# A trunk of two layers: rounded transposes from word copies at the layer boundaries and in three more MLP clusters

## The chip, the cores and the metric

One core of one Trainium2 chip runs the whole kernel in one launch. The metric is the device time of one execution in microseconds (us), as the median of several runs. Engines: TensorE (PE), its weight loads (PEld), VectorE (DVE), ScalarE (ACT), GpSimd (POOL), SyncE (SP).

## The reference

256 tokens of width 2048 go through two layers in fp32. Each layer is a mixer (latent attention, MLA, in the first; a state space mixer, SSM, in the second) and a squared-ReLU MLP of width 8192, each behind an RMS norm and added to the residual:

```python
def squared_relu_mlp(h, w_in, w_out):
    u = jax.nn.relu(h @ w_in)
    return (u * u) @ w_out

for i in range(DEPTH):
    h = rms_norm(x, mix_norm_g[i])
    mix = mla_mixer(h, ...) if i % N_MIXERS == 0 else ssm_mixer(h, ...)
    x = x + mix
    h = rms_norm(x, mlp_norm_g[i])
    x = x + squared_relu_mlp(h, mlp_w_in[i], mlp_w_out[i])
```

## The kernel before

**Products.** The 256 tokens are two row tiles (t = 0, 1) of 128. Every fp32 product is made of three fp32r matmuls of 128x512: each operand is split into a rounded part h (ScalarE's copy, L299 for activations and L102 for weights) and the rest lo (VectorE's subtraction, L300 and L103). A weight unit is 128x1024: SyncE loads it into a `wraw` buffer (6 of them), L102 and L103 make `wh` and `wl` (4 each), and twelve matmuls use it. `Flow` loads some units ahead and splits three ahead. A matmul needs the contracted dimension on the partitions, so each activation block is transposed on TensorE: four transposes of 128x128 into one PSUM bank (a cluster, `transposed`, L307), then L299 and L300.

**The two kinds of transposes.** L315 transposes fp32 data against an fp32 identity, `ident`. L313 transposes fp32r data (`words`) against the fp32r identity `identr`. For the latter, the first 384 columns of the block are copied, bytes unchanged, by a DMA of GpSimd's queue into an fp32r tile `tr` (L559); the fourth transpose stays fp32. Before, only MLP pairs 1 to 6 do this (`WORDS`).

**Boundaries.** There are three: MLA to MLP, MLP to SSM, SSM to MLP. A product's output comes in four column blocks (nb = 0 to 3). `finalize` adds a block to the residual (L399), multiplies it by the next norm's gain into a scratch tile xg (L401), takes the square sum on ScalarE (L296), and puts the transposes of xg into a queue with `later`. `tick` runs once per output block, that is about once per two weight units, and emits what has come due; `later(0)` is the next tick. At MLA to MLP and MLP to SSM the clusters alternate between two `yp` and two `sm` banks; at SSM to MLP they use `sm` alone (two banks). Column block 3 is the last of a boundary.

**The MLP.** Pairs 0 to 7 of hidden blocks (p): pair 0 is computed as it stands, pairs 1 to 7 by seven products of sums (`seven`). A pair gives four clusters (p, j, t): hidden block j of the pair, row tile t. The order of the units is a list made by `plan` and `merged`; the body walks it and counts estimated TensorE time in `at[0]`. `turn` puts a cluster into `due` at the earliest of its own delay (`TR`, plus `COPY` = 8 for a cluster with a copy) and at least `TR_GAP` = 4 us after the cluster before it. `move` emits the clusters that are due. After the last unit, `move(1e9)` emits all that are left. Then the four output blocks of pair 7 follow (`block`, matmuls L330, L331, L334), which end in `finalize`. `combinations` makes sums of the transposed input for the seven products (`xf`, L513 and L523) and splits them (`sN5`, `sN7`, `sN6`). `seven` adds raw weight tiles on VectorE (L183) and in HBM-to-buffer loads that accumulate on GpSimd's queue (L199). All other matmuls of the MLP are L605, L606, L607; L424 adds an output block to the residual in `x`.

Of the kernel before, what the change touches and what calls it, by code (L numbers as in the profile page):

```python
# [20 lines left out]
F32 = mybir.dt.float32  # L21
F32R = mybir.dt.float32r
# [6 lines left out]
P = 128  # L29
# [9 lines left out]
NEG = -1.0e30  # L39
MAGIC = 12582912.0  # L40

C_ID, C_G0, C_GQ, C_GK, C_MQ, C_TRI, C_SEL = 0, 128, 144, 336, 528, 656, 784
C_INV, C_DTB, C_ALOG, C_CW, C_CB, C_END = 848, 880, 944, 1008, 1200, 1248


def inv_two_pi_parts():
# [168 lines left out]
class Trunk:  # L215
# [82 lines left out]
    def split_out(self, h, lo, src):  # L298
        self.nc.scalar.activation(h, src, AF.Copy)  # L299
        self.nc.vector.tensor_tensor(lo, src, h.bitcast(F32), ALU.subtract)  # L300

    def transposes(self, src, h, lo, t, wide=True):

        sl = slice(t * P, (t + 1) * P)
        self.transposed(src, h[:, :, sl], lo[:, :, sl], wide)

    def transposed(self, src, h, lo, wide=True):  # L307
        b = self.bank(wide)
        src, words = src if isinstance(src, tuple) else (src, None)
        for j in range(4):  # L310
            v = slice(j * P, (j + 1) * P)
            if words is not None and j < 3:
                self.nc.tensor.transpose(b.bitcast(F32R)[:, v], words[:, v], self.ident_r)  # L313
            else:
                self.nc.tensor.transpose(b[:, v], src[:, v], self.ident)  # L315
        self.split_out(h, lo, b.rearrange("p (k n) -> p k n", k=4))
# [67 lines left out]
    def finalize(self, nb, accs, wide=True):  # L384
        nc = self.nc
        g = self.gain_tile(self.nx_gain[nb])
        if not self.by_tile:
            self.nx[nb] = (self.ktile(self.xtp), self.ktile(self.xtp))
        elif nb % 2 == 0:
            for t in range(2):  # L390
                self.nx[nb // 2, t] = [self.ktile(self.xtp).rearrange("p a b -> p (a b)").rearrange("p (k n) -> p k n", n=P)
                                       for _ in range(2)]
        for t in range(2):
            if self.by_tile:
                h, lo = (v[:, 4 * (nb % 2):4 * (nb % 2) + 4] for v in self.nx[nb // 2, t])
            else:
                h, lo = (v[:, :, t * P:(t + 1) * P] for v in self.nx[nb])
            x = self.x[t][nb]
            nc.vector.tensor_tensor(x, accs[t], x, ALU.add)  # L399
            xg = self.scratch()  # L400
            nc.vector.tensor_tensor(xg, x, g, ALU.mult)  # L401
            self.square_sum(x, self.nx_ssq[:, t * 4 + nb:t * 4 + nb + 1])
            self.later(0, lambda h=h, lo=lo, xg=xg: self.transposed(xg, h, lo, wide))

    def boundary_end(self):

# [20 lines left out]
    def start(self, seq):  # L427
        nc, d = self.nc, self.d
        self.flow = Flow(nc, self.wp, seq, (6, 3))
        cst = self.c.tile([P, C_END], F32, name="cst")  # L430
        self.cst = cst
        self.ident = cst[:, C_ID:C_ID + P]
        self.mhalf = self.c.tile([P, 16], F32, name="mhalf")
        warm = self.s2.tile([P, 512], F32R, tag="s2", name="warm")
        nc.vector.memset(warm.bitcast(F32), 1.0)
        bank = self.sm.tile([P, 512], F32, tag="sm", name="warmed")
        for _ in range(WARM):
            nc.tensor.matmul(bank, warm[:, :P], warm, start=True, stop=True)
        nc.gpsimd.memset(self.mhalf, -0.5)
        nc.scalar.dma_start(cst[:, C_G0:C_GQ], d["cst"][:, C_G0:C_GQ])  # L440
        nc.scalar.activation(self.stat(1), self.mhalf[:, :1], AF.Copy)
        raws = [self.ktile(self.k4, F32) for _ in range(4)]
        parts = [(0, slice(k, k + 1)) for k in range(4)] + [(1, slice(0, 2)), (1, slice(2, 4)), (2, slice(0, 4)), (3, slice(0, 4))]

        def some_x():
            j, k = parts.pop(0)
            nc.sync.dma_start(raws[j][:, k], d["xT"][j][:, k])

        self.flow.load(2, ((0, 512), (512, 1024)), some_x)
        for u in range(3, 7):  # L450
            some_x()
            self.flow.load(u)
        self.pos = self.c.tile([P, 2], I32, name="pos")
        self.x = [[self.res.tile([P, 512], F32, name=f"x{t}{n}") for n in range(4)] for t in range(2)]

        self.rs_pool = [self.c.tile([P, 4], F32, name=f"rs{i}") for i in range(2)]
        self.phase = 0
        self.xT = [(self.ktile(self.xtp), self.ktile(self.xtp)) for _ in range(4)]

        def split_x(j, ks):  # L460
            h, lo = self.xT[j]
            for k in ks:
                g = cst[:, C_G0 + 4 * j + k:C_G0 + 4 * j + k + 1]
                if (j, k) == (0, 0):
                    nc.vector.tensor_scalar(h[:, k], raws[j][:, k], g, None, ALU.mult)
                else:
                    nc.scalar.activation(h[:, k], raws[j][:, k], AF.Copy, scale=g)
                nc.vector.scalar_tensor_tensor(lo[:, k], raws[j][:, k], g, h[:, k].bitcast(F32), ALU.mult, ALU.subtract)  # L468

        split_x(0, (0,))  # L470
        self.flow.convert(1)
        split_x(0, (1, 2))
        self.flow.convert(2)
        split_x(0, (3,))
        self.flow.load(7)
        nc.sync.dma_start(cst[:, :C_G0], d["cst"][:, :C_G0])
        nc.sync.dma_start(cst[:, C_GQ:], d["cst"][:, C_GQ:])
        nc.sync.dma_start(self.pos, d["pos"])
        split_x(1, range(4))
        ssq = self.stat(8)  # L480
        self.later(0, lambda: split_x(2, range(4)))
        self.later(1, lambda: split_x(3, range(4)))

        def stats(n):
            for t in range(2):
                nc.sync.dma_start(self.x[t][n], d["x"][t * P:(t + 1) * P, n * 512:(n + 1) * 512])
                self.square_sum(self.x[t][n], ssq[:, t * 4 + n:t * 4 + n + 1])
            if n == 3:
                self.set_rstd(ssq)

        for n, at in enumerate(X_AT):
            self.later(at, lambda n=n: stats(n))
# [51 lines left out]
    def mlp_body(self, mp, layer, gain):  # L544
        nc = self.nc
        xa, rs = self.xT, self.rs
        us = {}
        self.ident_r = mp.tile([P, P], F32R, name="identr")
        nc.gpsimd.tensor_copy(self.ident_r, self.ident)

        def hidden(r, pp, j, t):

            nc.scalar.activation(r, r, AF.Square)
            if (pp, j) not in us:
                us[pp, j] = (self.ktile(self.k4), self.ktile(self.k4))
            h, lo = us[pp, j]
            if pp in WORDS:
                q = mp.tile([P, 384], F32R, tag="tr", name=self.name("tr"), bufs=4)
                nc.gpsimd.dma_start(q.bitcast(F32), r[:, :384])  # L559
                r = (r, q)  # L560
            return lambda wide: self.transposes(r, h, lo, t, wide)

        def relu(src, t):
# [14 lines left out]
        at = [0.0, 0.0]  # L578
# [10 lines left out]
        def turn(r, p, j, t, us):  # L589

            fn = hidden(r, p, j, t)
            at[1] = max(at[0] + us + (COPY if p in WORDS else 0), at[1] + TR_GAP)
            due.append((at[1], lambda: fn(False)))

        def pair_of_banks(pool):
# [49 lines left out]
        for tok in tokens:  # L645
            key = (tok[0], layer) + tok[1:]
            if tok[0] == "s":
                _, p, name, d = tok
# [3 lines left out]
                if count.setdefault(name, 0) % 4 == 0:  # L652
                    pool = self.sm if name == "N7" else self.acc
# [7 lines left out]
            elif tok[0] == "c":  # L661
                _, p, j, o = tok
# [11 lines left out]
            else:  # L674
                _, p, nb, o = tok
# [701 lines left out]
LATE5 = ()  # L1377
TR = (10, 8, 7, 7, 5)
TR_GAP = 4
WORDS = range(1, 7)  # L1380
COPY = 8
PAUSE = 2.7


def merged(p, blocks):
# [21 lines left out]
    while main or late or second or units:  # L1407
        op = next((q for q in (late, main, second) if q and ready(*q[0])), None)
        filler = t >= rest and len(units) > (4 if p == 7 and op else 0)
        if filler and (op is None or work > t * ve / pe - 2):  # L1410
# [3 lines left out]
            if not units or units[0][0] != b:  # L1414
                rest, work = t + (PAUSE if b[0] == "o" else 10), work + 1.37
        else:
# [160 lines left out]
```

## Time and profile before

| | |
|---|---|
| three runs | 2288.47, 2289.15, 2289.5 us; median 2289.15 |
| profiled execution | own time 2289.32 us, span 2287.5 us, clock 1.0 |
| fp32 transposes (L315) | 288, of these 252 into `sm` and 36 into `yp` |
| word transposes (L313) | 144, from 48 copies of 192 KB |
| DMA | 547.52 MB, mean 239 GB/s |

In the profile, a row of the timeline gives the start, the length, the engine, the line, the operation, output<-input and how many instructions in a row it groups (x4); in brackets stands the idle time before it and what ended it. A matmul's length reaches into the next one's, since they are pipelined: the pace is the distance of their starts. Rows of a view by source line give the count, then minimum, median and maximum duration in ns.

### The profile page before, as it was taken

The page shows a single profiled execution, that of the slowest core. Times are in us where ns is not written, and L with a number is a line of the kernel's source. Part 1 is how long each engine was busy: PE and PEld are TensorE (multiplying, and loading weights), DVE is VectorE, ACT ScalarE, POOL GpSimd, SP SyncE. Part 2 cuts the span into 40 slices and gives each one's busy share as a digit, 9 for nine tenths or more (in the row PEclk, how much of TensorE's full clock was granted, in tenths as well). Part 3 has the DMA queues.
Part 4 walks back from the last instruction along what each step waited for, and adds up shares of the span by engine and source line. Part 5 has one row for each costly group of instructions (what it writes and reads, how often), then busy time and mean ns, then how long its engine had stood idle before and what let it go on. Part 6 is the DMA issues. An engine that isn't in the chain of part 4 may idle for free.

```text
span 2287.5 us, 30624 instructions
## 1 busy us (share of the span) xinstructions
PE 2280.0 (100%) x10929; PEld 1893.7 (83%) x10929; DVE 1906.0 (83%) x2318; ACT 1391.2 (61%) x1947; POOL 243.0 (11%) x279
## 2 busy tenths in 40 slices
PE   9999999999999999999999999999999999999999
PEld 7898888888888888888888888888888888888887
DVE  7785698999898897687888688676989989989985
ACT  7775476566566666564666555544666666666663
POOL 1430000000000000000133112110000000000000
PEclk9999999999999999999999999999999999999999
DMA  8435678888888878667877777666688888888875
GB/s 316 151 125 152 202 228 266 261 257 267 265 253 259 268 231 271 202 207 241 279 270 261 251 265 259 221 200 202 208 266 240 267 269 253 261 277 244 267 230 161
DMA packets 164985, 547.52 MB, mean 239 GB/s; under 512 B 18448, under 2 KB 27600, under 8 KB 163808
## 3 DMA queue, kind: packets, MB, share of 16 engines
q1 hardware_dynamic: 151264, 502.44, 66.4%
q0 software_dynamic: 11168, 38.85, 9.0%
q10 hardware_dynamic: 2400, 4.27, 0.5%
q8 instruction: 86, 1.41, 0.2%
q14 instruction: 67, 0.55, 0.1%
HBM read 529.65 MB, written 6.41 MB: 234 GB/s over the span
## 4 chain that ended last, share of the span: by engine, by line
PE 95%; DVE 2%; DMA 2%; ACT 1%; issue 1%; POOL 0%; SPq 0%; ACTq 0%; DVEq 0%
PE acc L330 13%; PE acc L331 13%; PE acc L334 13%; PE yp L606 9%; PE yp L607 9%; PE yp L605 9%; PE st L606 7%; PE st L607 7%; PE st L605 7%; DMA wraw<-mi 1%; PE sm L315 1%; DVE wl L103 1%; PE y L1291 1%; PE acc L607 1%; PE acc L605 1%
## 5 line engine op out<-in xcount | busy, mean ns | idle before, releaser
L102 ACT ACTIVATE wh<-wraw 128x1024 fp32r<-128x1024 f32 (+1 forms) x818 | 856.7, 1053 | 582.3 <-PE acc L331 287.9
L103 DVE TENSOR_TENSOR wl<-wraw,wh 128x1024 fp32r<-128x1024 f32 (+1 forms) x818 | 983.3, 1219 | 230.8 <-ACT wh L102 221.8
L605 PE MATMUL yp<-wh,k 128*128 128x512 f32 x896 | 349.3, 390 | 0.0
L607 PE MATMUL yp<-wh,k 128*128 128x512 f32 x896 | 349.1, 390 | 0.0
L606 PE MATMUL yp<-wl,k 128*128 128x512 f32 x896 | 348.9, 389 | 0.0
L330 PE MATMUL acc<-wh,xt 128*128 128x512 f32 x704 | 279.2, 397 | 1.0 <-ACT wh L102 1.0
L331 PE MATMUL acc<-wh,xt 128*128 128x512 f32 x704 | 274.6, 390 | 0.3 <-DVE xt L468 0.3
L102 ACT ACTIVATE wh<-wrx 128x1024 fp32r<-128x1024 f32 x168 | 177.8, 1058 | 153.7 <-PE yp L607 102.9
L103 DVE TENSOR_TENSOR wl<-wrx,wh 128x1024 fp32r<-128x1024 f32 x168 | 204.1, 1220 | 36.4 <-ACT wh L102 35.5
L606 PEld LDWEIGHTS yp<-wl,k 128*128 128x128 f32 x896 | 168.2, 188 | 35.1 <-DVE wl L103 0.4
L607 PEld LDWEIGHTS yp<-wh,k 128*128 128x128 f32 x896 | 168.2, 188 | 35.1
L605 PEld LDWEIGHTS yp<-wh,k 128*128 128x128 f32 x896 | 168.3, 188 | 34.7
L330 PE MATMUL acc<-wh,k 128*128 128x512 f32 x496 | 196.6, 396 | 0.0
L331 PE MATMUL acc<-wh,k 128*128 128x512 f32 x496 | 193.2, 390 | 0.0
L334 PE MATMUL acc<-wl,xt 128*128 128x512 f32 x704 | 188.3, 389 | 0.0
L605 PE MATMUL st<-wh,xt 128*128 128x512 f32 x448 | 177.4, 396 | 0.0
L607 PE MATMUL st<-wh,xt 128*128 128x512 f32 x448 | 174.9, 390 | 0.0
L606 PE MATMUL st<-wl,xt 128*128 128x512 f32 x448 | 174.9, 390 | 0.0
L330 PEld LDWEIGHTS acc<-wh,xt 128*128 128x128 f32 x704 | 132.2, 188 | 29.8 <-ACT wh L102 1.9
L331 PEld LDWEIGHTS acc<-wh,xt 128*128 128x128 f32 x704 | 132.3, 188 | 28.5 <-issue 1.2
L334 PEld LDWEIGHTS acc<-wl,xt 128*128 128x128 f32 x704 | 132.2, 188 | 27.6
L334 PE MATMUL acc<-wl,k 128*128 128x512 f32 x496 | 132.7, 389 | 0.0
(311 smaller groups left out, 3399.4 us busy)
## 6 DMA issues: line engine op xcount, KB each, us to landing
wraw<-mi SPq DMA_DIRECT2D x256, 512.0 KB, 5.5
wraw<-mo SPq DMA_DIRECT2D x256, 512.0 KB, 5.4
wraw<-si SPq DMA_DIRECT2D x160, 512.0 KB, 4.9
wraw<-so SPq DMA_DIRECT2D x64, 512.0 KB, 4.8
wrx<-mi SPq DMA_DIRECT2D x56, 512.0 KB, 5.1
wrx<-mi POOLq DMA_DIRECT2D x56, 512.0 KB, 7.6
wraw<-wo SPq DMA_DIRECT2D x32, 512.0 KB, 4.2
taps<-xD SPq DMA_DIRECT2D x16, 768.0 KB, 8.6
```

The costliest lines, as they stand in the source:

```text
L102: self.last = nc.scalar.activation(h[:, v], raw[:, v], AF.Copy)
L103: self.last_lo = nc.vector.tensor_tensor(lo[:, v], raw[:, v], h[:, v].bitcast(F32), ALU.subtract)
L315: self.nc.tensor.transpose(b[:, v], src[:, v], self.ident)
L330: nc.tensor.matmul(accs[t][:, :n], ah, wh[:, q, :], start=first and kt + q == 0, stop=False)
L331: nc.tensor.matmul(accs[t][:, :n], al, wh[:, q, :], start=False, stop=False)
L334: nc.tensor.matmul(accs[t][:, :n], lhs(kt + q, t)[0], wl[:, q, :], start=False, stop=en and q == nk - 1)
L605: nc.tensor.matmul(b, ah, wh, start=first and q == 0, stop=False)
L606: nc.tensor.matmul(b, ah, wl, start=False, stop=False)
L607: nc.tensor.matmul(b, al, wh, start=False, stop=last and q == 1)
L1291: nc.tensor.matmul(y[t][c, o], part(t)[:, c], xg[g][t][:, o], start=True, stop=True)
```

## The change

`words` is a new helper: it copies the first n x 128 columns of a block into an fp32r tile by a DMA of GpSimd's queue. `finalize` uses it for column blocks 0 to 2: all four transposes of row tile 0 and three of row tile 1 become fp32r, and both row tiles' clusters are emitted one tick later than before (`later(1)`). Column block 3 is as before. The copies of the boundaries live in the scratch pool `s2`. In the MLP, clusters (0,0,0), (0,0,1) and (7,1,1) get a copy as well, and with it the 8 us of `COPY` in their due time. The identity is one fp32r tile for the whole kernel, loaded at the start through a scratch tile; its fp32 view is `ident`, and the two copies of it at the MLPs' starts go. After the change the lines are some ten further down: L324 is the fp32 transpose, L322 the one from words, L308 the copy, L339, L340 and L343 the matmuls of `block`, L615 to L617 those of the MLP, L408 and L410 `finalize`, L527 and L537 `combinations`.

```diff
--- before.py
+++ after.py
@@ -39,8 +39,8 @@
 NEG = -1.0e30
 MAGIC = 12582912.0
 
-C_ID, C_G0, C_GQ, C_GK, C_MQ, C_TRI, C_SEL = 0, 128, 144, 336, 528, 656, 784
-C_INV, C_DTB, C_ALOG, C_CW, C_CB, C_END = 848, 880, 944, 1008, 1200, 1248
+C_G0, C_GQ, C_GK, C_MQ, C_TRI, C_SEL = 0, 16, 208, 400, 528, 656
+C_INV, C_DTB, C_ALOG, C_CW, C_CB, C_END = 720, 752, 816, 880, 1072, 1120
 
 
 def inv_two_pi_parts():
@@ -299,6 +299,15 @@
         self.nc.scalar.activation(h, src, AF.Copy)
         self.nc.vector.tensor_tensor(lo, src, h.bitcast(F32), ALU.subtract)
 
+    def words(self, src, n, pool=None):
+
+        if pool:
+            q = pool.tile([P, n * P], F32R, tag="tr", name=self.name("tr"), bufs=4)
+        else:
+            q = self.s2.tile([P, 512], F32R, tag="s2", name=self.name("tr"))[:, :n * P]
+        self.nc.gpsimd.dma_start(q.bitcast(F32), src[:, :n * P])
+        return src, q, n
+
     def transposes(self, src, h, lo, t, wide=True):
 
         sl = slice(t * P, (t + 1) * P)
@@ -306,10 +315,10 @@
 
     def transposed(self, src, h, lo, wide=True):
         b = self.bank(wide)
-        src, words = src if isinstance(src, tuple) else (src, None)
+        src, words, n = src if isinstance(src, tuple) else (src, None, 0)
         for j in range(4):
             v = slice(j * P, (j + 1) * P)
-            if words is not None and j < 3:
+            if j < n:
                 self.nc.tensor.transpose(b.bitcast(F32R)[:, v], words[:, v], self.ident_r)
             else:
                 self.nc.tensor.transpose(b[:, v], src[:, v], self.ident)
@@ -400,7 +409,9 @@
             xg = self.scratch()
             nc.vector.tensor_tensor(xg, x, g, ALU.mult)
             self.square_sum(x, self.nx_ssq[:, t * 4 + nb:t * 4 + nb + 1])
-            self.later(0, lambda h=h, lo=lo, xg=xg: self.transposed(xg, h, lo, wide))
+            if nb < 3:
+                xg = self.words(xg, 4 - t)
+            self.later(int(nb < 3), lambda h=h, lo=lo, xg=xg: self.transposed(xg, h, lo, wide))
 
     def boundary_end(self):
 
@@ -429,7 +440,8 @@
         self.flow = Flow(nc, self.wp, seq, (6, 3))
         cst = self.c.tile([P, C_END], F32, name="cst")
         self.cst = cst
-        self.ident = cst[:, C_ID:C_ID + P]
+        self.ident_r = self.c.tile([P, P], F32R, name="ident")
+        self.ident = self.ident_r.bitcast(F32)
         self.mhalf = self.c.tile([P, 16], F32, name="mhalf")
         warm = self.s2.tile([P, 512], F32R, tag="s2", name="warm")
         nc.vector.memset(warm.bitcast(F32), 1.0)
@@ -473,7 +485,9 @@
         self.flow.convert(2)
         split_x(0, (3,))
         self.flow.load(7)
-        nc.sync.dma_start(cst[:, :C_G0], d["cst"][:, :C_G0])
+        one = self.scratch()
+        nc.sync.dma_start(one[:, :P], d["one"])
+        nc.gpsimd.tensor_copy(self.ident_r, one[:, :P])
         nc.sync.dma_start(cst[:, C_GQ:], d["cst"][:, C_GQ:])
         nc.sync.dma_start(self.pos, d["pos"])
         split_x(1, range(4))
@@ -545,8 +559,6 @@
         nc = self.nc
         xa, rs = self.xT, self.rs
         us = {}
-        self.ident_r = mp.tile([P, P], F32R, name="identr")
-        nc.gpsimd.tensor_copy(self.ident_r, self.ident)
 
         def hidden(r, pp, j, t):
 
@@ -554,10 +566,8 @@
             if (pp, j) not in us:
                 us[pp, j] = (self.ktile(self.k4), self.ktile(self.k4))
             h, lo = us[pp, j]
-            if pp in WORDS:
-                q = mp.tile([P, 384], F32R, tag="tr", name=self.name("tr"), bufs=4)
-                nc.gpsimd.dma_start(q.bitcast(F32), r[:, :384])
-                r = (r, q)
+            if by_words(pp, j, t):
+                r = self.words(r, 3, mp)
             return lambda wide: self.transposes(r, h, lo, t, wide)
 
         def relu(src, t):
@@ -589,7 +599,7 @@
         def turn(r, p, j, t, us):
 
             fn = hidden(r, p, j, t)
-            at[1] = max(at[0] + us + (COPY if p in WORDS else 0), at[1] + TR_GAP)
+            at[1] = max(at[0] + us + (COPY if by_words(p, j, t) else 0), at[1] + TR_GAP)
             due.append((at[1], lambda: fn(False)))
 
         def pair_of_banks(pool):
@@ -1377,8 +1387,12 @@
 LATE5 = ()
 TR = (10, 8, 7, 7, 5)
 TR_GAP = 4
-WORDS = range(1, 7)
 COPY = 8
+
+
+def by_words(p, j, t):
+
+    return 0 < p < 7 or (p, j) == (0, 0) or (p, j, t) == (7, 1, 1)
 PAUSE = 2.7
 
 
@@ -1562,8 +1576,9 @@
     taps = np.concatenate([f(ssm_conv_w)[0], f(ssm_conv_b)], 0)[:, :4096]
     a["cwx"] = rows(taps.reshape(5, 8, 512).transpose(1, 0, 2), 2560)
     cw = f(ssm_conv_w)[0].reshape(4, 48, P).transpose(2, 1, 0).reshape(P, 192)
+    a["one"] = np.eye(P, dtype=np.float32)
     a["cst"] = np.ascontiguousarray(np.concatenate([
-        np.eye(P, dtype=np.float32), f(mix_norm_g)[0].reshape(16, P).T, rep(f(mla_qk_norm_q)[0]), rep(f(mla_qk_norm_k)[0]),
+        f(mix_norm_g)[0].reshape(16, P).T, rep(f(mla_qk_norm_q)[0]), rep(f(mla_qk_norm_k)[0]),
         upper * np.float32(NEG), np.triu(one), sel, rep(inv), rep(f(ssm_dt_bias)[0]),
         rep(f(ssm_a_log)[0]), cw, f(ssm_conv_b)[0].reshape(48, P).T], axis=1, dtype=np.float32))
     assert a["cst"].shape[1] == C_END
```

How the order moves, at the places that matter. TensorE at the end of the first MLP, before: the last matmuls of an output block (`yp`), the cluster (7,1,0) and the first matmuls of pair 7's output block, whose operands `k4_646` and `k4_647` (h and lo of hidden block 0) come from two earlier clusters.

```order
L606 MATMUL yp_652_8292<-wl404_8296,k4_610_7373 128x512
L607 MATMUL yp_652_8292<-wh404_8295,k4_611_7374 128x512
L315 MATMUL sm_654_8374<-cst_96,s2_641_8128 128x128 x4
L330 MATMUL acc_656_8382<-wh405_8313,k4_646_8208 128x512
L331 MATMUL acc_656_8382<-wh405_8313,k4_647_8209 128x512
L330 MATMUL acc_657_8383<-wh405_8313,k4_646_8208 128x512
L331 MATMUL acc_657_8383<-wh405_8313,k4_647_8209 128x512
L330 MATMUL acc_656_8382<-wh405_8313,k4_646_8208 128x512
```

The same place after: `sm_663` is (7,0,1), `sm_664` is (7,1,0), and `k4_656` and `k4_657` are h and lo of hidden block 0, whose row tile 1 comes from `sm_663`.

```order
L616 MATMUL yp_660_8297<-wl404_8301,k4_619_7390 128x512
L617 MATMUL yp_660_8297<-wh404_8300,k4_620_7391 128x512
L324 MATMUL sm_663_8386<-ident_97,s2_649_8144 128x128 x4
L324 MATMUL sm_664_8393<-ident_97,s2_650_8145 128x128 x4
L339 MATMUL acc_666_8401<-wh405_8325,k4_656_8227 128x512
L340 MATMUL acc_666_8401<-wh405_8325,k4_657_8228 128x512
L339 MATMUL acc_667_8402<-wh405_8325,k4_656_8227 128x512
L340 MATMUL acc_667_8402<-wh405_8325,k4_657_8228 128x512
L339 MATMUL acc_666_8401<-wh405_8325,k4_656_8227 128x512
L340 MATMUL acc_666_8401<-wh405_8325,k4_657_8228 128x512
```

The cluster (7,0,1) moved one unit down and now stands right ahead of the block that reads it.

TensorE at SSM to MLP, before: the cluster pair of column block 3, between two units of the MLP's pair 0 (`wh647`, `wh648`). The pair of column block 2 stands two units up, ahead of unit 646.

```order
L606 MATMUL acc_1009_14776<-wl647_14695,xt_970_14476 128x512
L607 MATMUL acc_1009_14776<-wh647_14694,xt_971_14477 128x512
L315 MATMUL sm_1010_14809<-cst_96,s2_1001_14745 128x128 x4
L315 MATMUL sm_1011_14816<-cst_96,s2_1003_14750 128x128 x4
L605 MATMUL acc_1008_14775<-wh648_14712,xt_968_14474 128x512
L606 MATMUL acc_1008_14775<-wl648_14713,xt_968_14474 128x512
L607 MATMUL acc_1008_14775<-wh648_14712,xt_969_14475 128x512
L605 MATMUL acc_1009_14776<-wh648_14712,xt_970_14476 128x512
```

The same place after: `sm_1030` and `sm_1031` are column block 2, row tiles 0 and 1; `sm_1032` and `sm_1033` are column block 3.

```order
L617 MATMUL acc_1029_14803<-wh647_14737,xt_987_14508 128x512
L322 MATMUL sm_1030_14836<-ident_97,tr_1016_14726 128x128 x4
L322 MATMUL sm_1031_14843<-ident_97,tr_1019_14733 128x128 x3
L324 MATMUL sm_1031_14843<-ident_97,s2_1017_14729 128x128
L324 MATMUL sm_1032_14850<-ident_97,s2_1021_14774 128x128 x4
L324 MATMUL sm_1033_14857<-ident_97,s2_1023_14779 128x128 x4
L615 MATMUL acc_1028_14802<-wh648_14755,xt_984_14505 128x512
L616 MATMUL acc_1028_14802<-wl648_14756,xt_984_14505 128x512
```

Four clusters now stand in a row, on two banks.

VectorE some instructions behind them, before: the splits of the weights (`wl653` and on), the sums `xf` of the transposed input and the splits `sN`; L183 is the sum of raw weight tiles. The split `wl652` stands in the row above these.

```order
L523 TENSOR_TENSOR xf_1014_14827<-xf_1012_14823,xf_1014_14827 128x1024
L103 TENSOR_TENSOR wl653_14886<-wraw653_14852,wh653_14885 128x1024
L523 TENSOR_TENSOR xf_1012_14823<-xf_1012_14823,xf_1013_14825 128x1024
L300 TENSOR_TENSOR sN5_1016_14831<-xf_1014_14827,sN5_1015_14830 128x1024
L523 TENSOR_TENSOR xf_1013_14825<-xf_1013_14825,xf_1014_14827 128x1024
L300 TENSOR_TENSOR sN7_1018_14872<-xf_1012_14823,sN7_1017_14871 128x1024
L523 TENSOR_TENSOR xf_1021_14880<-xf_1021_14880,xf_1013_14825 128x1024
L300 TENSOR_TENSOR sN6_1020_14877<-xf_1013_14825,sN6_1019_14876 128x1024
L103 TENSOR_TENSOR wl654_14904<-wraw654_14883,wh654_14903 128x1024
L103 TENSOR_TENSOR wl655_14922<-wraw655_14901,wh655_14921 128x1024
L103 TENSOR_TENSOR wl656_14942<-wrx656_14919,wh656_14941 128x1024
L183 TENSOR_TENSOR wraw657_14939<-wraw657_14937,wraw657_14939 128x1024
```

The same after, from the first sum `xf` that needs column block 3:

```order
L527 TENSOR_TENSOR xf_1036_14868<-xt_1012_14719,xt_1013_14720 128x1024
L183 TENSOR_TENSOR wraw657_14980<-wraw657_14978,wraw657_14980 128x1024
L537 TENSOR_TENSOR xf_1036_14868<-xf_1034_14864,xf_1036_14868 128x1024
L103 TENSOR_TENSOR wl652_14896<-wraw652_14875,wh652_14895 128x1024
L537 TENSOR_TENSOR xf_1034_14864<-xf_1034_14864,xf_1035_14866 128x1024
L300 TENSOR_TENSOR sN5_1038_14872<-xf_1036_14868,sN5_1037_14871 128x1024
L537 TENSOR_TENSOR xf_1035_14866<-xf_1035_14866,xf_1036_14868 128x1024
L300 TENSOR_TENSOR sN7_1040_14913<-xf_1034_14864,sN7_1039_14912 128x1024
L537 TENSOR_TENSOR xf_1043_14921<-xf_1043_14921,xf_1035_14866 128x1024
L300 TENSOR_TENSOR sN6_1042_14918<-xf_1035_14866,sN6_1041_14917 128x1024
L103 TENSOR_TENSOR wl653_14927<-wraw653_14893,wh653_14926 128x1024
L103 TENSOR_TENSOR wl654_14945<-wraw654_14924,wh654_14944 128x1024
```

L183 of `wraw657` moved from behind `wl656` to ahead of `wl652`, and `wl653` moved behind the three splits `sN`.

## The prediction

> **What bounds the kernel now.** I read the page's busy shares and the chain that ended last, then the list of waits on TensorE, then the timeline of each place that the change touches. From the page, busy time by engine, the chain, and how the copies on GpSimd's queue land (the second fence, from the view of tile `tr`):
> ```profile
> PE 2280.0 (100%) x10929; PEld 1893.7 (83%) x10929; DVE 1906.0 (83%) x2318; ACT 1391.2 (61%) x1947; POOL 243.0 (11%) x279
> PE 95%; DVE 2%; DMA 2%; ACT 1%; issue 1%; POOL 0%; SPq 0%; ACTq 0%; DVEq 0%
> ```
> ```profile
> L559 POOL DMA_DIRECT2D tr<-s x48: 536/552/590, 364.1 to 2150.1; - x48
> DMA to landing us min/median/max: 2.1/5.1/7.2
> ```
> TensorE is busy for 2280.0 of 2287.5 us and 95% of the chain is its own work. So whatever shortens TensorE's stream shortens the kernel, and whatever makes TensorE wait lengthens it by the whole wait; nothing else counts. DVE stands at 83% on average, and at the places below it has no gap at all. The profiled execution's own time is 2289.32 us (its span and 1.8 us around it), 0.17 above the median of 2289.15; the sum is made against 2289.3.
>
> **The gain: 81 transposes.** The change turns 63 transposes at three boundaries (3 column blocks, 4 + 3 each) and 18 in the MLPs (2 layers, 3 clusters, 3 each) from fp32 into rounded words. The two kinds by source line, duration as minimum, median and maximum in ns, and then TensorE's timeline around a cluster of four fp32 and around one of three words and one fp32:
> ```profile
> L315 PE MATMUL sm<-cst,s x252: 269/272/298, 49.2 to 2240.1; 128*128 128x128 f32 x126
> L313 PE MATMUL sm<-identr,tr x144: 222/227/249, 375.6 to 2160.4; 128*128 128x128 f32 x144
> ```
> ```profile
> 1635.50 0.40 PE L607 MATMUL yp<-wh,xt 128*128 128x512 f32 x1
> 1635.73 0.60 PE L315 MATMUL sm<-cst,s 128*128 128x128 f32 x4
> 1636.09 0.47 PE L605 MATMUL yp<-wh,xt 128*128 128x512 f32 x1
> 1636.40 0.39 PE L606 MATMUL yp<-wl,xt 128*128 128x512 f32 x1
> ...
> 2155.32 0.39 PE L606 MATMUL yp<-wl,k 128*128 128x512 f32 x1
> 2155.54 0.40 PE L607 MATMUL yp<-wh,k 128*128 128x512 f32 x1
> 2155.78 0.37 PE L313 MATMUL sm<-identr,tr 128*128 128x128 f32 x3
> 2155.98 0.30 PE L315 MATMUL sm<-cst,s 128*128 128x128 f32 x1
> 2156.04 0.48 PE L605 MATMUL st<-wh,sN 128*128 128x512 f32 x1
> 2156.35 0.39 PE L606 MATMUL st<-wl,sN 128*128 128x512 f32 x1
> ```
> Matmuls overlap, so a cluster's cost is read from the start of the matmul ahead of it to the second one behind it, less two ordinary steps of some 0.227 us (2155.32 to 2155.54 is one): 0.90 - 0.45 = 0.45 us with four fp32, 0.81 - 0.45 = 0.36 with three words. Three words save 0.09 us, one saves 0.03, and 81 save **2.4 us**. The medians of duration differ by more, 45 ns; that would make 3.6 us, and is the upper end. By either, the gain cannot reach 0.2% (4.6 us), which is about what a measurement of this kernel can tell from no change.
>
> [...]
>
> **Loss one: the end of each MLP (about 3.2 us for two layers).** Cluster (7,1,1) now waits for a copy: its due time is 8 us later, and each later cluster follows its predecessor by at least 4 us. As the order shows, (7,0,1) and (7,1,0) now stand back to back directly ahead of the output block of pair 7, whose third and fourth matmuls read what (7,0,1) gives. Before, one cluster stood there, and its result was needed only four units on. The end of the first MLP before, TensorE, ScalarE and VectorE (each by its timeline):
> ```profile
> 903.05 0.60 PE L315 MATMUL sm<-cst,s 128*128 128x128 f32 x4
> 903.41 0.48 PE L330 MATMUL acc<-wh,k 128*128 128x512 f32 x1
> 903.73 0.39 PE L331 MATMUL acc<-wh,k 128*128 128x512 f32 x1
> ```
> ```profile
> 903.25 1.06 ACT L102 ACTIVATE wh<-wraw 128x1024 fp32r<-128x1024 f32 x1 [1.66 <-PE yp L607]
> 904.22 0.58 ACT L299 ACTIVATE k<-sm 128x512 fp32r<-128x512 f32 x1
> ```
> ```profile
> 902.76 1.28 DVE L424 TENSOR_TENSOR x<-yp,x 128x512 f32<-128x512 f32 x2
> 904.35 1.23 DVE L103 TENSOR_TENSOR wl<-wraw,wh 128x1024 fp32r<-128x1024 f32 x1 [0.30 <-ACT wh L102]
> 905.49 0.68 DVE L300 TENSOR_TENSOR k<-sm,k 128x512 fp32r<-128x512 f32 x1
> ```
> Call the start of the first transpose X (903.05). VectorE's split of the cluster, L300, ends at 906.17, X + 3.1, because the split of a weight tile, L103, stands ahead of it, and that waits for ScalarE's L102, which the last unit's end releases. In the changed order the same instructions stand in the same order in front of the split that is now needed. Two clusters take 0.9 us, so the block's fourth matmul could start at X + 0.36 + 0.45 + three steps of 0.23 to 0.32, about X + 1.55; it waits until X + 3.15: **1.6 us, twice, 3.2**. If DVE were free it would still wait for L299 and one L300, which leaves about 0.45 us each (0.9 in all); at the top I allow 1.8 each. Behind the waiting matmul on TensorE stands everything, so nothing covers it.
>
> **Loss two: SSM to MLP (about 5.2 us).** Here the transposes of a column block use only the two `sm` banks. Blocks 2 and 3 stood a unit pair apart (X = 1615.67 is block 3's); a tick later, block 2's stand directly ahead of block 3's. So block 3's two clusters wait for the two splits of block 2 that free the banks. Before, by timeline, with the one load that matters from the view of SyncE's issues of `wraw` at 1618:
> ```profile
> 1615.67 1.03 PE L315 MATMUL sm<-cst,s 128*128 128x128 f32 x8
> 1616.46 0.48 PE L605 MATMUL acc<-wh,xt 128*128 128x512 f32 x1
> ...
> 1633.10 0.46 PE L606 MATMUL yp<-wl,xt 128*128 128x512 f32 x1
> ```
> ```profile
> 1616.96 1.23 DVE L103 TENSOR_TENSOR wl<-wraw,wh 128x1024 fp32r<-128x1024 f32 x1 [1.42 <-ACT wh L102]
> 1618.10 1.28 DVE L300 TENSOR_TENSOR xt<-sm,xt 128x512 fp32r<-128x512 f32 x2
> 1619.30 2.35 DVE L513 TENSOR_TENSOR xf<-xt,xt 128x1024 f32<-128x1024 f32 x2
> 1621.57 1.22 DVE L103 TENSOR_TENSOR wl<-wraw,wh 128x1024 fp32r<-128x1024 f32 x1
> 1622.70 1.22 DVE L523 TENSOR_TENSOR xf<-xf,xf 128x1024 f32<-128x1024 f32 x1
> 1623.84 1.22 DVE L103 TENSOR_TENSOR wl<-wraw,wh 128x1024 fp32r<-128x1024 f32 x1
> ```
> ```profile
> L85 SPq DMA_DIRECT2D wraw<-mi x1: 328/328/328, 1618.2 to 1618.2; - x1
> DMA to landing us min/median/max: 6.5/6.5/6.5
> ```
> First wait: L300 of block 2 stands behind L103 (1616.96), starts at X + 2.4 and frees a bank at X + 3.1, the second at X + 3.7. Block 3's last cluster starts at X + 3.75 and the next matmul at X + 4.1. Without a wait four clusters take about 1.57 us and that matmul starts at X + 1.48: **2.6 us**. Second wait: in the changed order the sum of a raw weight tile (L183 of `wraw657`) stands ahead of the split `wl652`, and three splits of activations stand between `wl652` and `wl653`. L183 needs the load issued at 1618.2, that is X + 2.5, which lands 6.5 later, at X + 9.05, while VectorE is through with what stands ahead by X + 8.0 (block 3's splits end 1.5 after its last cluster, at X + 5.65, then two instructions, 2.35). From L183 to `wl653` are ten instructions; their steps are 1.135 us (1621.57, 1622.70, 1623.84), so `wl653` ends at X + 9.05 + 9 x 1.135 + 1.22 = X + 20.5. TensorE wants it at the second matmul of its sixth unit from there: X + 4.1 + 5 x 2.72 + 0.23 = X + 17.95 (a unit is 12 steps). **2.55 us**; had the load landed by X + 8.0, 1.5; with 7.2, 3.2. Together 5.2, between 4.1 and 5.8. Behind it `wl654` ends at X + 21.6, over a microsecond before its unit, so the loss stops there.
>
> **What should cost nothing.** The 24 new copies each take 0.55 us of GpSimd, which is idle for 89% of the span, and their use is one tick (two units, 5.4 us) later. The tightest is row tile 1 at the MLA boundary, where xg now stands behind a weight split:
> ```profile
> 222.89 1.28 DVE L401 TENSOR_TENSOR s<-x,gb 128x512 f32<-128x512 f32 x2
> 223.77 1.06 ACT L102 ACTIVATE wh<-wraw 128x1024 fp32r<-128x1024 f32 x1
> 227.16 0.60 PE L315 MATMUL yp<-cst,s 128*128 128x128 f32 x4
> ```
> L102 ends at 224.8, the split takes 1.2, xg 0.7: the copy is issued at 226.75 and lands after the median of 5.1 at 231.85; its transposes start at 227.16 + 5.44 + 0.33 = 232.9. One microsecond is left; with the slowest landing, 7.2, TensorE would wait for 1.05. I take nothing, and keep up to 3 us (three column blocks) for the range. [...] The MLP's clusters (0,0) are only needed two units or more after their new place; the tick's other delays (an xg buffer held longer, the gain load behind raw loads) end on buffers that come free before their next writer. The identity is loaded and copied at the start, before any transpose needs it: nothing within some tenths of a microsecond either way.
>
> **The sum.** 2289.3 - 2.4 + 3.2 + 5.2 = **2295.3 us**, +0.26%. Own range with the bounds above: 2289.3 - 3.6 + 0.9 + 4.1 = 2290.7 to 2289.3 - 2.4 + 3.6 + 5.8 = 2296.3.
>
> **The rivals.**
> - All waits hidden, only the gain shows: 2286.9, not slower. Its place is the two clusters ahead of the output block and the four at the SSM boundary; it decides if VectorE reaches L300 within about 1.5 us of X. For it speaks that before loses nothing there; against it the 3.1 us from X to L300's end. Chance 0.10.
> - One wait is much shorter: `wl653` in time because the load lands early and VectorE catches up, or the MLP ends wait only for ScalarE. 2289.3 - 2.4 + 2.6 + 0.9 to 3.2 = 2290.4 to 2292.7, middle 2291.5. Chance 0.18: the load's landing is one row.
> - Copies late at the boundaries as well: 1 us at two or three places, 2297.3, up to 2298.3. For it the maximum of 7.2, against it the median of 5.1. Chance 0.12.
> - [...] Chance 0.02.
>
> **How the numbers follow.** The forecast keeps 0.58, of which some 0.06 lie below 2293.7. Within 0.2%: 0.10 + 0.18 + 0.06 = 0.34; slower 0.52 + 0.12 = 0.64; faster 0.02. Forecast, second and third rival hold 0.88, so the range runs from 2290.0 to 2298.3.
>
> **What would show it.** In the changed trace TensorE's waits should name VectorE's L300 ahead of L340 at both MLP ends (1.6 us each) and ahead of the fp32 transposes at the SSM boundary (2.6 in all), then VectorE's L103 ahead of L616 (2.55), and no waits on copies. A cluster of four words should cost near 0.33 us. The prediction is wrong if these waits are missing or if TensorE waits for DMAs at L322.

## The result and the profile after

The changed kernel takes 2297.0 us (median of 7 runs, 2295.61 to 2298.03) against 2289.5 for the kernel before (7 runs): a ratio of 1.0033, 95% interval 1.0023 to 1.0043. It is slower by about 7.5 us; 6.0 were forecast. The profiled execution took 2297.0 us, with a span of 2294.9 against 2287.5.

From the page of the changed kernel, busy time by engine; then its list of waits on TensorE (total us, number, longest), whose `warmed` row, 1.4 us at the start, stands in the kernel before as well:

```profile
PE 2282.4 (99%) x10929; PEld 1892.8 (82%) x10929; DVE 1907.6 (83%) x2318; ACT 1392.2 (61%) x1947; POOL 255.0 (11%) x302
```
```profile
PE sm L324 <- DVE xt L300: 2.3, 1, 2.3
PE acc L340 <- DVE k L300: 1.7, 2, 0.9
PE warmed L450 <- DVE warm L447: 1.4, 1, 1.4
PE st L616 <- DVE wl L103: 1.0, 2, 0.7
PE acc L616 <- DVE wl L103: 0.7, 1, 0.7
PE acc L339 <- ACT k L299: 0.6, 2, 0.3
...
PE sm L322 <- DVE k L300: 0.4, 1, 0.4
```

The first, the second and the fifth are the waits that were forecast; no row names a copy. TensorE's busy time is up by 2.4 us (2282.4 against 2280.0) although its transposes got cheaper: a sign of a slower clock, which is 0.54 in one stretch below.

Both kernels have the same 9408 matmuls (9216 of 128x512, the others 128x384) in the two helpers that run MLP and projections, in the same order, so each can be paired with its counterpart, and the shift of its start can be read. The table shows how the shift grows from stage to stage, in us, in the profiled execution of each kernel; stages go by the times of the kernel before:

| stage | from, to | changed kernel | forecast |
|---|---|---|---|
| start and MLA | 0, 225 | +0.21 | 0 |
| MLA to MLP, 21 words | 225, 270 | -0.54 | -0.63 |
| first MLP up to its end, 6 words | 270, 880 | +0.23 | -0.2 |
| end of the first MLP, 3 words | 880, 912 | +1.60 | +1.6 - 0.1 |
| MLP to SSM, 21 words | 912, 970 | -0.56 | -0.63 |
| SSM | 970, 1580 | +0.03 | 0 |
| SSM to MLP, column blocks 0 and 1 | 1580, 1599 | -0.39 | -0.42 |
| SSM to MLP, column blocks 2 and 3 | 1599, 1633 | +4.93 | +5.2 - 0.2 |
| second MLP's start, 6 words | 1633, 1656 | +0.31 | -0.2 |
| second MLP | 1656, 2215 | -0.02 | 0 |
| end of the second MLP, 3 words | 2215, 2262 | +1.64 | +1.6 - 0.1 |
| sum | | +7.44 | +6.0 |

The end of the first MLP after the change, TensorE and VectorE by timeline:

```profile
902.40 1.03 PE L324 MATMUL sm<-ident,s 128*128 128x128 f32 x8
903.19 0.48 PE L339 MATMUL acc<-wh,k 128*128 128x512 f32 x1
903.50 0.40 PE L340 MATMUL acc<-wh,k 128*128 128x512 f32 x1
904.20 0.50 PE L339 MATMUL acc<-wh,k 128*128 128x512 f32 x1 [0.29 <-ACT k L299]
905.57 0.50 PE L340 MATMUL acc<-wh,k 128*128 128x512 f32 x1 [0.87 <-DVE k L300]
```
```profile
903.69 1.22 DVE L103 TENSOR_TENSOR wl<-wraw,wh 128x1024 fp32r<-128x1024 f32 x1 [0.19 <-ACT wh L102]
904.83 1.28 DVE L300 TENSOR_TENSOR k<-sm,k 128x512 fp32r<-128x512 f32 x2
```

With X = 902.40, the fourth matmul starts at X + 3.17 (3.15 in the forecast), right behind the first of the two L300, which stand behind the weight split L103. The brackets (0.29 and 0.87) are idle time alone; since matmuls overlap (0.40 us long, an ordinary step from start to start 0.23), the loss is read from the starts: 903.50 to 905.57 are two steps of 0.23 and 1.6 us of waiting.

SSM to MLP after the change, TensorE and VectorE by timeline, and TensorE's granted clock there (stretch, length, busy us and matmuls, clock, DMA share, GB/s):

```profile
1615.38 0.71 PE L322 MATMUL sm<-ident,tr 128*128 128x128 f32 x7
1615.92 0.29 PE L324 MATMUL sm<-ident,s 128*128 128x128 f32 x1
1618.55 1.82 PE L324 MATMUL sm<-ident,s 128*128 128x128 f32 x8 [2.33 <-DVE xt L300]
1620.02 0.78 PE L615 MATMUL acc<-wh,xt 128*128 128x512 f32 x1
1620.60 0.63 PE L616 MATMUL acc<-wl,xt 128*128 128x512 f32 x1
1621.02 0.63 PE L617 MATMUL acc<-wh,xt 128*128 128x512 f32 x1
...
1622.24 0.40 PE L617 MATMUL acc<-wh,xt 128*128 128x512 f32 x1
1622.48 0.39 PE L615 MATMUL acc<-wh,xt 128*128 128x512 f32 x1
...
1635.76 0.50 PE L616 MATMUL acc<-wl,xt 128*128 128x512 f32 x1 [0.65 <-DVE wl L103]
```
```profile
1616.67 1.23 DVE L103 TENSOR_TENSOR wl<-wraw,wh 128x1024 fp32r<-128x1024 f32 x1 [1.49 <-ACT wh L102]
1617.81 1.28 DVE L300 TENSOR_TENSOR xt<-sm,xt 128x512 fp32r<-128x512 f32 x2
...
1624.26 1.23 DVE L183 TENSOR_TENSOR wraw<-wraw,wraw 128x1024 f32<-128x1024 f32 x1 [0.26 <-DMA wraw<-mi]
...
1634.48 3.49 DVE L103 TENSOR_TENSOR wl<-wraw,wh 128x1024 fp32r<-128x1024 f32 x3
```
```profile
1615.00:1618.50 3.50, 1.21 (x11) 1.00 0.76 239
1618.50:1622.20 3.70, 3.65 (x13) 0.54 0.81 242
1622.20:1626.00 3.80, 3.80 (x18) 1.00 0.22 87
```

With X = 1615.38, block 3's transposes start at X + 3.17 and the matmul behind them at X + 4.64 (forecast 4.1). VectorE waits 0.26 us for the load that L183 needs and starts it at X + 8.88 (forecast 9.05), and `wl653` ends at 1634.48 + 1.22 = X + 20.3 (forecast 20.5). What was not forecast: behind the gap of 2.33 us the clock is 0.54, and matmuls start every 0.43 us in place of 0.23.

### The profile page after: what moved, and what is told of

Read it like the earlier page. It is cut to its first block, busy times and chain, and to the rows that moved or that the text cites. A ratio compares the mean times of both kernels' runs of the same rounds, so it can differ in the third digit from the quotient of the medians.

```text
span 2294.9 us, 30713 instructions
## 1 busy us (share of the span) xinstructions
PE 2282.4 (99%) x10929; PEld 1892.8 (82%) x10929; DVE 1907.6 (83%) x2318; ACT 1392.2 (61%) x1947; POOL 255.0 (11%) x302
## 5 line engine op out<-in xcount | busy, mean ns | idle before, releaser
L102 ACT ACTIVATE wh<-wraw 128x1024 fp32r<-128x1024 f32 (+1 forms) x818 | 856.9, 1053 | 588.2 <-PE acc L340 283.3
L103 DVE TENSOR_TENSOR wl<-wraw,wh 128x1024 fp32r<-128x1024 f32 (+1 forms) x818 | 985.0, 1221 | 236.6 <-ACT wh L102 226.8
L615 PE MATMUL yp<-wh,k 128*128 128x512 f32 x896 | 349.2, 390 | 0.0
L617 PE MATMUL yp<-wh,k 128*128 128x512 f32 x896 | 348.8, 389 | 0.0
L339 PE MATMUL acc<-wh,xt 128*128 128x512 f32 x704 | 279.8, 397 | 0.5 <-ACT wh L102 0.5
L340 PE MATMUL acc<-wh,xt 128*128 128x512 f32 x704 | 275.0, 391 | 0.0
L102 ACT ACTIVATE wh<-wrx 128x1024 fp32r<-128x1024 f32 x168 | 177.8, 1059 | 153.3 <-PE yp L617 99.8
L103 DVE TENSOR_TENSOR wl<-wrx,wh 128x1024 fp32r<-128x1024 f32 x168 | 204.5, 1222 | 35.0 <-ACT wh L102 34.4
L339 PE MATMUL acc<-wh,k 128*128 128x512 f32 x496 | 196.7, 397 | 0.6 <-ACT k L299 0.6
L617 PEld LDWEIGHTS yp<-wh,k 128*128 128x128 f32 x896 | 168.2, 188 | 35.1
L615 PEld LDWEIGHTS yp<-wh,k 128*128 128x128 f32 x896 | 168.3, 188 | 34.8
L340 PE MATMUL acc<-wh,k 128*128 128x512 f32 x496 | 193.4, 390 | 1.7 <-DVE k L300 1.7
L343 PE MATMUL acc<-wl,xt 128*128 128x512 f32 x704 | 188.3, 389 | 0.0
L615 PE MATMUL st<-wh,xt 128*128 128x512 f32 x448 | 177.5, 396 | 0.0
L617 PE MATMUL st<-wh,xt 128*128 128x512 f32 x448 | 174.8, 390 | 0.0
L339 PEld LDWEIGHTS acc<-wh,xt 128*128 128x128 f32 x704 | 132.6, 188 | 29.3 <-ACT wh L102 1.4
L340 PEld LDWEIGHTS acc<-wh,xt 128*128 128x128 f32 x704 | 132.5, 188 | 28.5 <-issue 1.2
L343 PEld LDWEIGHTS acc<-wl,xt 128*128 128x128 f32 x704 | 132.2, 188 | 27.6
L615 PE MATMUL st<-wh,sN 128*128 128x512 f32 x336 | 133.2, 396 | 0.0
```

What stands on the lines that cost most here:

```text
L102: self.last = nc.scalar.activation(h[:, v], raw[:, v], AF.Copy)
L103: self.last_lo = nc.vector.tensor_tensor(lo[:, v], raw[:, v], h[:, v].bitcast(F32), ALU.subtract)
L339: nc.tensor.matmul(accs[t][:, :n], ah, wh[:, q, :], start=first and kt + q == 0, stop=False)
L340: nc.tensor.matmul(accs[t][:, :n], al, wh[:, q, :], start=False, stop=False)
L343: nc.tensor.matmul(accs[t][:, :n], lhs(kt + q, t)[0], wl[:, q, :], start=False, stop=en and q == nk - 1)
L615: nc.tensor.matmul(b, ah, wh, start=first and q == 0, stop=False)
```

## The experiments

All times are medians, each with its ratio to the kernel before, which was timed beside it (2289.49 in the first four, 2289.46 in the last four), and the ratio's interval. The stages are those of the table above, read from each run's profiled execution. Theory: two separate groups of waits on VectorE, each made by clusters that now stand back to back. Rivals: VectorE is late by itself, or the copies are what costs.

**1. The boundaries alone.**

```diff
-    return 0 < p < 7 or (p, j) == (0, 0) or (p, j, t) == (7, 1, 1)
+    return 0 < p < 7
```

> The boundaries as in the change (words and the tick), the MLP clusters as before. Theory: the loss is two separate groups of waits on VectorE. Here the MLP ends lose nothing, 63 word transposes gain 1.75 us, the SSM boundary keeps its two waits and the slow clock after the first (5.1 us): about 2292.7 us, 3.3 above before, and the wait of the changed kernel at the second MLP's start on a bank is gone or not according to whether it comes from the MLP clusters. Rival: the MLP ends wait because the whole stream on VectorE is later through the boundaries; then TensorE waits 1.6 us at each MLP end here too.

2293.5 us, ratio 1.0020 (1.0011 to 1.0028). No wait on L300 ahead of L340 is left; the wait for the bank is the same 2.3 us:

```profile
PE sm L324 <- DVE xt L300: 2.3, 1, 2.3
PE st L616 <- DVE wl L103: 1.7, 3, 0.7
```

By shifts, column blocks 2 and 3 of the SSM boundary add 5.0 us (from -1.34 at 1599 to +3.68 at 1633), and the MLP ends 0.06 and 0.04. So the MLP ends' waits come from the MLP's own clusters. The profiled execution loses another 1.83 us in the second MLP (run 3 loses 1.79 there, the changed kernel nothing), where it waits for two weight splits, 1.4 us in all (part of the `st` row). What delays them was not tested.

**2. The MLP clusters alone.**

```diff
-            if nb < 3:
-                xg = self.words(xg, 4 - t)
-            self.later(int(nb < 3), lambda h=h, lo=lo, xg=xg: self.transposed(xg, h, lo, wide))
+            self.later(0, lambda h=h, lo=lo, xg=xg: self.transposed(xg, h, lo, wide))
```

> The boundaries as before, the three MLP clusters per layer by words as in the change. Theory: 18 word transposes gain 0.55 us, each MLP end waits 1.6 us for the split of (7,0,1), the SSM boundary loses nothing: about 2289.3 - 0.55 + 3.3 = 2292.1 us. Rival: the waits of the MLP ends need the boundaries' changes as well; then about 2288.8 us.

2293.81 us, ratio 1.0016 (1.0007 to 1.0025), 1.7 above the expectation in the median (the profiled span is 4.5 us longer than before's). The MLP ends add 1.64 and 1.63, the SSM boundary nothing (+2.48 at 1599, +2.46 at 1633). The two groups are separate. The excess stands inside the two MLPs, +0.83 in the first and +0.61 in the second, partly as short waits for weight splits (`st` L103, 0.9 us in three, where the kernel before has 0.7 in two) and for a bank ahead of a cluster by words (0.6 in two). It can't be assigned further: the changed kernel, run 4 and run 7 execute the same instructions up to the SSM boundary, and their first MLPs add +0.23, +0.50 and -0.50.

**3. The tick without words.**

```diff
-    return 0 < p < 7 or (p, j) == (0, 0) or (p, j, t) == (7, 1, 1)
+    return 0 < p < 7
...
-            if nb < 3:
-                xg = self.words(xg, 4 - t)
```

> Only the tick: column blocks 0 to 2 are transposed a tick later, in fp32 and without copies; the MLP clusters as before. Theory: the SSM boundary loses the same through the banks, whatever the kind of transposes: 2289.3 + 5.1 = 2294.4 us, 1.75 above the boundaries with words, with TensorE idle for about 2.1 us ahead of column block 3's transposes. Rival: the copies and what they hold on VectorE or in buffers cause the loss; then within 1 us of 2289.3.

2295.44 us, ratio 1.0026 (1.0015 to 1.0036): slower without a single copy at the boundaries. The boundary adds 5.18 us between 1599 and 1633. Its waits, and the clock around the wait for a bank, the second row (L614 is this kernel's `wl` matmul):

```profile
PE acc L614 <- DVE wl L103: 2.3, 1, 2.3
PE sm L324 <- DVE xt L300: 2.1, 1, 2.1
```
```profile
1616.50:1618.00 1.50, 0.03 (x1) 1.00 0.69 251
1618.00:1620.00 2.00, 2.00 (x13) 1.00 0.67 152
```

The copies are not the cause. Here the clock stays at 1.00 behind the gap of 2.14 us, and the wait for `wl653` is 2.3 in place of 0.7; the boundary's loss is the same.

**4. Four banks.**

```diff
-                        self.finalize(nb, accs[nb], False)
+                        self.finalize(nb, accs[nb], nb > 1)
```

> The change, with one edit: at SSM to MLP column blocks 2 and 3 use the two yp banks as well, so that their four clusters have four banks. Theory: the wait for a bank goes, with it the slow clock, and VectorE's order comes back to that of before (weights ahead of sums): 5.1 us less than the change, about 2292 us; only the MLP ends (3.3) and the second MLP's start (0.5) still lose. Rival: VectorE is late by itself at that place, and TensorE then waits behind the four clusters for the splits or the weights: within 1.5 us of the changed kernel, 2297.

2291.49 us, ratio 1.0011 (1.0002 to 1.0020). TensorE at the place, and then VectorE: its order is that of before again, with `wl652` and `wl653` (the first row) ahead of the splits `sN` (the second):

```profile
1615.00 0.45 PE L322 MATMUL yp<-ident,tr 128*128 128x128 f32 x4
1615.29 0.42 PE L322 MATMUL sm<-ident,tr 128*128 128x128 f32 x3
1615.55 0.29 PE L324 MATMUL sm<-ident,s 128*128 128x128 f32 x1
1615.68 0.60 PE L324 MATMUL yp<-ident,s 128*128 128x128 f32 x4
1616.11 0.60 PE L324 MATMUL sm<-ident,s 128*128 128x128 f32 x4
1616.47 0.48 PE L615 MATMUL acc<-wh,xt 128*128 128x512 f32 x1
```
```profile
1624.37 1.22 DVE L103 TENSOR_TENSOR wl<-wraw,wh 128x1024 fp32r<-128x1024 f32 x1
...
1626.64 1.22 DVE L300 TENSOR_TENSOR sN<-xf,sN 128x1024 fp32r<-128x1024 f32 x1
```

The next matmul starts at X + 1.47, as the forecast had it without a wait, and the stage from 1599 to 1633 gives -0.18 in place of +4.93. One changed argument undoes both waits: the bank is the cause of the first, and the order in which VectorE's work is laid out, the cause of the second, follows from the bank as well.

**5. Four banks, and (7,1,1) as before.** Edit of 4, and

```diff
-    return 0 < p < 7 or (p, j) == (0, 0) or (p, j, t) == (7, 1, 1)
+    return 0 < p < 7 or (p, j) == (0, 0)
```

> The change with four banks at SSM to MLP for column blocks 2 and 3, and with cluster (7,1,1) back in fp32 without a copy or its delay; (0,0,0) and (0,0,1) stay by words. Theory: with both groups of waits gone only the gain and the wait at the second MLP's start (0.5) are left: 3.2 less than the run with four banks, about 2287.9 us, and no wait on L300 ahead of the output block. Rival: the output block waits whichever cluster stands last, because VectorE is behind at the end of an MLP; then TensorE still waits over 1 us there and the time stays near 2291.

2289.62 us, ratio 0.9999 (0.9990 to 1.0007); the profiled span is 2286.5, 1.0 below before's. The MLP ends add 0.02 and 0.01. The loss is gone, and so is the wait. The gain that was expected beyond that, 1.5 us below the kernel before, does not show in the medians, whose interval reaches from 2.3 us below it to 1.6 above.

**6. Words without the tick.** MLP clusters as before, and

```diff
-            self.later(int(nb < 3), lambda h=h, lo=lo, xg=xg: self.transposed(xg, h, lo, wide))
+            self.later(0, lambda h=h, lo=lo, xg=xg: self.transposed(xg, h, lo, wide))
```

> The boundaries by words, but all column blocks at the next tick as before; MLP clusters as before. Theory: the copies land 5 us after their issue, row tile 1's copy is issued 3 us after the block's end, and the transposes stand 5.4 us after it, so TensorE waits on the copy at each of the nine column blocks, 3 to 4.5 us each, and longer than the 2.3 us after which the clock fell in the changed kernel, which adds about 1 us each: 2315 to 2340 us, the middle 2330. Rival: copies that nothing else competes with land in about 2.5 us; then 1 to 2 us each, about 2303.

2327.49 us, ratio 1.0164 (1.0150 to 1.0178). TensorE's list of waits, the landing of all its copies, and the clock before and behind one of the gaps:

```profile
PE sm L322 <- DMA tr<-s: 26.0, 9, 3.6
```
```profile
DMA to landing us min/median/max: 2.1/4.8/6.9
```
```profile
931.20:934.70 3.50, 0.08 (x1) 1.00 0.95 335
934.70:939.00 4.30, 4.22 (x14) 0.61 0.28 106
```

Eight waits of 2.6 to 3.6 us and a short one make 26.0, less each than expected, and one of the nine places hardly waits. Of the rest of the 37 us most is left to the slow clock: it is 0.61 behind the gap above, and 0.994 in the mean of the whole execution, where the kernel before has 1.0. The total is close to the expected middle. So the tick is what the copies need, and its price at one boundary is what the change paid.

**7. The gap filled.**

```diff
+    def fill(self):
+
+        b = self.yp.tile([P, 512], F32, tag="yp", name=self.name("fill"))
+        for _ in range(10):
+            self.nc.tensor.matmul(b, self.ident_r, self.nx[0, 0][0][:, 0:4], start=True, stop=True)
...
+            if nb == 3 and t == 0 and not wide:
+                self.later(0, self.fill)
```

> The change, with ten matmuls of 128x512 into a spare bank, read by nothing, put ahead of column block 3's transposes at SSM to MLP, where TensorE is idle for 2.33 us. Theory: the clock stays at 1.0, so the transposes and matmuls behind the gap are 1.3 us faster, and the wait for the weight split wl653 grows by the same, since that split ends by VectorE's own chain: the time stays at 2297 us within 0.5. Rival: the slow clock is a loss of its own; then about 1.3 us less than the changed kernel, 2295.7.

2297.05 us, ratio 1.0033 (1.0021 to 1.0046): unchanged. TensorE there (`wl` matmuls are L624 in this kernel):

```profile
1614.97 2.57 PE L422 MATMUL fill<-xt,ident 128*128 128x512 f32 x10
1617.55 1.25 PE L324 MATMUL sm<-ident,s 128*128 128x128 f32 x8
1618.55 0.48 PE L623 MATMUL acc<-wh,xt 128*128 128x512 f32 x1
1618.87 0.40 PE L624 MATMUL acc<-wl,xt 128*128 128x512 f32 x1
...
1635.06 0.50 PE L624 MATMUL acc<-wl,xt 128*128 128x512 f32 x1 [2.39 <-DVE wl L103]
```

The eight transposes take 1.00 us to the next matmul's start where they took 1.47, the clock is 1.00 and the steps are 0.23 us again, and the wait for `wl653` grows from 0.65 to 2.39, by 1.7 where 1.3 was expected. In the changed kernel the slow clock costs nothing of its own: it fills time in which TensorE would wait for VectorE.

**8. (7,1,1) by words, in a slot of its own.** Edit of 4, (0,0) as before, and in `turn`:

```diff
+            if (p, j, t) == (7, 1, 1):
+                due.append((at[0] + us + COPY, lambda: fn(False)))
+                return
```

> The boundaries by words with four banks at SSM to MLP, clusters (0,0) in fp32 as before, and (7,1,1) by words with its 8 us of delay but without pushing the clusters behind it. Theory: (7,0,1) keeps its place a unit ahead of the output block, and the MLP ends lose nothing although the copy is there: 2289.3 - 1.75 - 0.2 = 2287.4 us, no wait on L300 ahead of L340. Rival: the copy of (7,1,1) itself makes the block wait; then over 1 us of waits on a DMA or on the split behind it, at each MLP end.

2288.66 us, ratio 0.9998 (0.9989 to 1.0007); the profiled span is 2285.6, 1.9 below before's. The MLP ends add -0.05 and -0.01 with the copy in place, so it was the push on the clusters behind it, not the copy. The median is 1.3 above the expectation. This is the lowest of all, some 8 us below the changed kernel, and not to be told from the kernel before by its runs.

## Why the prediction was right

- **The gain** was 2.4 us in the forecast. Column blocks 0 to 2 show it: the pair of clusters takes 0.60 us to the next matmul's start (926.78 to 927.38) where fp32 took 0.79 (902.40 to 903.19).

```profile
926.78 0.46 PE L322 MATMUL yp<-ident,tr 128*128 128x128 f32 x4
927.08 0.41 PE L322 MATMUL sm<-ident,tr 128*128 128x128 f32 x3
...
927.38 0.48 PE L339 MATMUL acc<-wh,k 128*128 128x512 f32 x1
```

  That is 0.19 for seven, 0.027 each where 0.030 was taken, and 2.2 us for 81. The chance of 0.02 for faster would need a transpose to save several times that, which no run shows. The sum rightly did not use the difference of the durations (45 ns).
- **The MLP ends** were forecast at 3.2 and measure 1.60 + 1.64, with the place, the engine and the chain as told (L102, L103, L300).
- **SSM to MLP** was forecast at 5.2 and measures 4.93, or 5.1 without the seven words' gain. The place and the engine were right, the split into two steps was not. The first step has the wait for the bank that was forecast (2.6), but the forecast lacks the slow clock behind it: the next matmul starts 0.5 later than told, and the slow steps after it add 1.0. The second was 2.55 in the forecast and 0.9 measured, since TensorE came 1.6 later to a split that ended when it was forecast to. That the two errors cancel is no luck: both steps end on one chain of VectorE, at X + 20.3, and runs 3 and 7, whose profiled executions show a clock of 1.0, add 5.18 and 5.24.
- **No copy is late**: no run with the tick has a wait on `tr`. In the changed kernel the copies land 5.0 us after their issue in the median, 6.9 at most.
- **The step that failed** is "what should cost nothing", at one place. The MLPs' starts were forecast to gain 0.2 each by the clusters (0,0); the second one lost 0.31. There the second of the two clusters waits for a bank, until VectorE has split the first one:

```profile
1654.26 0.44 PE L322 MATMUL sm<-ident,tr 128*128 128x128 f32 x3 [0.38 <-DVE k L300]
```

  By the starts it loses 0.6 us. Run 7 has this wait again (+0.39 for the stage). Run 1, with the MLP clusters of before, does not (-0.11), nor does run 2, with the boundaries of before (-0.15). So it stands there only where the clusters by words and the loss at the boundary come together; by what path the one reaches the other stays open, and run 2 has a shorter wait of this kind (0.2) at the first MLP's start. Runs 4, 5 and 8 add +0.31, +0.35 and +0.48 at the same stage by another wait, on a weight split right behind the boundary, which loses 0.46 by the starts and which the changed kernel does not have (in run 8):

```profile
PE yp L619 <- DVE wl L103: 0.3, 1, 0.3
```

- **What is chance**: forecast and measurement differ by 1.4 us, of which 0.5 is this step. Another 0.6 stands at the start (+0.21) and in the first MLP (+0.23 where -0.2 was forecast). The same instructions gave -0.42 and +0.50 there in run 4, -0.09 and -0.50 in run 7, so this part is no more than the spread between executions. The remaining 0.3 are the smaller gain of a word and the MLP ends.

## What to carry to other kernels

When TensorE is the bound, as here (99 to 100% busy), a cheaper form of its instruction is worth only its start-to-start difference, here 0.03 us a transpose, and one wait, here 1.6 us at an MLP's end, eats dozens of them. Before putting work a step later, look at what it will then stand next to: here clusters back to back shared two banks and the splitting engine, and that engine's queue decided when they went on (2.33 us of idle time at SSM to MLP). Where a delay belongs to one item, give it to that item alone and not to the chain of due times behind it.

## What the runs showed of the hardware

Behind some idle gaps of TensorE the granted clock was one half, behind others it was not, and the gap's length alone did not decide it. In the changed kernel a gap of 2.33 us was followed by 3.4 us at 0.50 (1618.75 to 1622.15, and 1.00 after it). In run 1 a gap of 2.33 us was followed by the slow clock as well (0.50 from 1618 to 1620), and in run 6 one of 3.50 us (0.61 from 934.70 to 939.00). A gap of 2.14 us in run 3, one of 2.39 in run 7 and one of 2.6 in run 6 were followed by 1.00, and run 3, with another gap of 2.3 us, has a mean clock of 1.0 over its whole profiled execution. What besides the length decides it was not shown.
